# Batched matmul on one core: groups of four matrices, one DMA queue for loads and stores, transposes of 32-bit pairs

## The chip, the cores and the metric

The kernel runs on one core of a Trainium2 chip. A core has a matrix engine (TensorE, "PE" in the profile), a vector engine (VectorE, "DVE"), a scalar engine (ScalarE, "ACT"), GpSimd ("POOL") and a sync engine (SyncE, "SP"), and 16 DMA engines that move data between HBM and the on-chip memory SBUF. Matmul results appear in PSUM, from where DVE or ACT copies them to SBUF. The metric is the device time of one execution in microseconds; the median of nine executions is given for the kernel before.

## What is computed

For each of 8 x 16 = 128 pairs of matrices the kernel forms one product of a 256 x 512 matrix with a 512 x 384 matrix, all in float32 in HBM:

```python
b1, b2, m, k, n = 8, 16, 256, 512, 384
x:      (b1, b2, m, k) float32
weight: (b1, b2, k, n) float32
return np.matmul(x, weight).astype(np.float32)
```

That is 67.1 MB of `x`, 100.7 MB of `weight` and 50.3 MB of output, 218.1 MB in all.

## The kernel before

The 128 products are worked off in groups: 63 groups of two matrices and, at the end, two groups of one. `GX` is 2, so one load of `x` always covers two matrices: `load_x` (line 58) brings 512 rows of `x` as 128 partitions with `R` = 4 consecutive rows each, which is one contiguous run of 8 KB per partition. `load_w` (line 65) brings one weight matrix as 128 partitions with four consecutive rows each, a run of 6 KB per partition. Because partition `p` of the weight tile holds rows 4p to 4p+3, the contraction is split by residue: step `ko` of the matmul takes the rows `ko`, `ko+4`, and so on. `x` is sliced in the same way (`ko::KO` on line 83).

TensorE needs `x` with the contraction on the partitions, so `transpose_x` (line 70) does three things per load: VectorE casts the float32 tile to bf16 (`x_bf`, line 77), TensorE transposes 128 x 128 blocks of it into PSUM (`pt`, line 82), and VectorE copies those to SBUF (`x_t`, line 86). The weights are cast to bf16 by VectorE (`w_bf`, line 110). In the main loop the two matrices of a group share the columns of the matrix engine: each matmul (line 124) has 64 columns of `x_t` as its stationary operand, matrix 0 writes partitions 0 to 63 of `po` and matrix 1 partitions 64 to 127. ScalarE copies `po` to `out_sb` (line 131), where each partition now holds `RG` = 4 consecutive output rows, a run of 6 KB.

The order of the work is set by the queues. All loads are issued from SP in program order. Stores are issued from ACT (`store`, line 95), and a list `waiting` holds each store back until `LAG` = 3 more groups have been computed. The framework gives DMAs eight completion semaphores in turn, so each DMA on SP also waits for the one that used the same semaphore before it: eight DMAs are under way at most, six loads and two stores in the steady state. Buffers are pools: three for the `x` tile, six for the weight tile, six for the output, two PSUM tiles for transposes and three for results. Each engine works off its own instructions in order; the framework has interleaved the instructions of neighbouring groups on VectorE and TensorE.

Of the kernel before, what the change touches and what calls it, by code (L numbers as in the profile page):

```python
# [1 line left out]

# [5 lines left out]


@with_exitstack
def kernel(
    ctx: ExitStack,
    tc: tile.TileContext,
    x: bass.AP,
    weight: bass.AP,
    out: bass.AP,
):
    nc = tc.nc
    P = 128  # L20

    b1, b2, M, K = x.shape
    _, _, _, N = weight.shape
    B = b1 * b2
    KO = K // P

    x_rows = x.rearrange("b1 b2 m k -> (b1 b2 m) k")
    o_rows = out.rearrange("b1 b2 m n -> (b1 b2 m) n")
    w_flat = weight.rearrange("b1 b2 k n -> (b1 b2) k n")

    fp32 = mybir.dt.float32
    bf16 = mybir.dt.bfloat16

    GX = 2
    CX = P // GX
    R = GX * M // P


    groups = [2] * ((B - GX) // 2) + [1] * GX

    LAG = 3

    const = ctx.enter_context(tc.tile_pool(name="const", bufs=1))
    x_pool = ctx.enter_context(tc.tile_pool(name="x_pool", bufs=3))
    xb_pool = ctx.enter_context(tc.tile_pool(name="xb_pool", bufs=2))
    xt_pool = ctx.enter_context(tc.tile_pool(name="xt_pool", bufs=2))
    w_pool = ctx.enter_context(tc.tile_pool(name="w_pool", bufs=6))
    wb_pool = ctx.enter_context(tc.tile_pool(name="wb_pool", bufs=4))  # L50
    out_pool = ctx.enter_context(tc.tile_pool(name="out_pool", bufs=LAG + 3))
    psum_t = ctx.enter_context(tc.tile_pool(name="psum_t", bufs=2, space=bass.MemoryType.PSUM))
    psum_o = ctx.enter_context(tc.tile_pool(name="psum_o", bufs=3, space=bass.MemoryType.PSUM))

    identity = const.tile([P, P], bf16)
    make_identity(nc, identity)

    def load_x(b):
        x_sb = x_pool.tile([P, R, K], fp32, name="x_sb")
        nc.sync.dma_start(  # L60
            x_sb[:], x_rows[b * M : (b + GX) * M].rearrange("(p r) k -> p r k", r=R)
        )
        return x_sb

    def load_w(b):
        w_sb = w_pool.tile([P, KO, N], fp32, name="w_sb")
        nc.sync.dma_start(w_sb[:], w_flat[b].rearrange("(kp ko) n -> kp ko n", ko=KO))  # L67
        return w_sb

    def transpose_x(x_sb, RG):  # L70


        H = R // RG
        x_bf = xb_pool.tile([P, R, K], bf16, name="x_bf")
        x_t = xt_pool.tile([P, RG, KO, P, H], bf16, name="x_t")
        for r0 in range(0, R, 4):
            nc.vector.tensor_copy(out=x_bf[:, r0 : r0 + 4], in_=x_sb[:, r0 : r0 + 4])  # L77
            for r in range(r0, r0 + 4, 2):
                pt = psum_t.tile([P, 2, KO, P], bf16, name="pt")
                for rr in range(2):  # L80
                    for ko in range(KO):
                        nc.tensor.transpose(  # L82
                            pt[:, rr, ko, :], x_bf[:, r + rr, ko::KO], identity
                        )
                j = r % RG
                nc.vector.tensor_copy(  # L86
                    out=x_t[:, j : j + 2, :, :, r // RG], in_=pt[:]
                )
        return x_t

    waiting = []

    def store():
        dram, out_sb = waiting.pop(0)
        nc.scalar.dma_start(out=dram, in_=out_sb)

    b = 0
    for n, G in enumerate(groups):
        last = n == len(groups) - 1
        C = P // G  # L100
        RG = G * M // P
        if b % GX == 0:
            x_sb = load_x(b)
        w_sb = [load_w(b + i) for i in range(G)]
        if b % GX == 0:
            x_t = transpose_x(x_sb, RG)
        w_bf = []
        for i in range(G):
            t = wb_pool.tile([P, KO, N], bf16, name="w_bf")
            nc.vector.tensor_copy(out=t[:], in_=w_sb[i][:])  # L110
            w_bf.append(t)
        if last:
            while waiting:
                store()

        out_full = out_pool.tile([P, 2 * M // P, N], fp32, name="out_sb")
        out_sb = out_full[:, :RG]
        for r in range(0, RG, 2):
            po = psum_o.tile([P, 2, 512], fp32, name="po")
            for rr in range(2):  # L120
                for ko in range(KO):
                    for i in range(G):
                        c0 = (b % GX + i) * CX
                        nc.tensor.matmul(  # L124
                            po[i * C : (i + 1) * C, rr, :N],
                            x_t[:, r + rr, ko, c0 : c0 + CX, :],
                            w_bf[i][:, ko, :],
                            start=(ko == 0),
                            stop=(ko == KO - 1),
                        )  # L130
            nc.scalar.copy(out=out_sb[:, r : r + 2, :], in_=po[:, :, :N])  # L131
        waiting.append(
            (
                o_rows[b * M : (b + G) * M].rearrange("(p r) n -> p r n", r=RG),
                out_sb,
            )
        )
        if len(waiting) > LAG or last:
            store()
        b += G  # L140


# [1 line left out]
_INS = ['x', 'weight']  # L144
_OUTS = [((8, 16, 256, 384), 'float32')]


# [23 lines left out]
```

## Time and profile before

| | |
|---|---|
| median of 9 executions | 531.84 us (530.17 to 534.15) |
| the profiled execution's own time | 530.17 us |
| its span in the profile | 528.0 us |
| PE busy | 346.8 us (66%) |
| DVE busy | 277.7 us (53%) |
| ACT busy | 103.8 us (20%) |
| granted TensorE clock, mean | 0.853 |
| HBM traffic over the span | 413 GB/s (167.77 MB read, 50.33 MB written) |

The span is the part of the execution that the profiler covers, from the first instruction to the last; the execution's own time is 2.17 us longer. Busy times are those of each engine on its own, and they overlap. A line of the profile that begins with a line number, an engine and an operation stands for a group of instructions of that kind: how many, their busy time, the mean of one in nanoseconds, and then how long the engine was idle just before them and what released it.

### The profile page before, as it was taken

What the parts mean: (1) busy time and instruction counts of PE and PEld (TensorE: products, weight loads), DVE (VectorE), ACT (ScalarE), POOL (GpSimd) and SP (SyncE); (2) the same over time, 40 slices, a digit from 0 to 9 for tenths busy, and PEclk for the clock granted to TensorE, in tenths of its full rate; (3) what the DMA queues carried; (4) which work ended last, traced back from release to release, by engine and by line L of the source; (5) the groups of instructions that cost most, each with busy time, mean ns of one, the idle gap of its engine ahead of it and who ended that gap; (6) DMA issues with size and microseconds to landing.
All of it is one profiled execution on the core that took longest, in us unless ns stands there. A gap on an engine that the chain in (4) does not pass through costs nothing.

```text
span 528.0 us, 7363 instructions
## 1 busy us (share of the span) xinstructions
PE 346.8 (66%) x3056; PEld 235.9 (45%) x3056; DVE 277.7 (53%) x320; ACT 103.8 (20%) x129; POOL 0.7 (0%) x6
## 2 busy tenths in 40 slices
PE   4685566675765766657667666576575775766664
PEld 2454344444543544445435444444454443544443
DVE  4545545555465545554654555546555455455464
ACT  0212111221211212212212122122221221112112
POOL 0000000000000000000000000000000000000000
PEclk9969888888788878887888888878888788788789
DMA  8999999999999999999999999999999999999994
GB/s 343 405 424 422 425 421 421 425 421 422 423 421 425 420 420 426 421 422 423 421 424 423 419 424 421 422 425 421 422 422 422 422 422 425 419 426 421 424 411 192
DMA packets 37041, 218.59 MB, mean 414 GB/s; under 512 B 4112, under 2 KB 4112, under 8 KB 28816
## 3 DMA queue, kind: packets, MB, share of 16 engines
q1 hardware_dynamic: 27648, 167.78, 76.4%
q10 hardware_dynamic: 9360, 50.34, 23.0%
q8 instruction: 24, 0.39, 0.3%
q14 instruction: 9, 0.07, 0.0%
HBM read 167.77 MB, written 50.33 MB: 413 GB/s over the span
## 4 chain that ended last, share of the span: by engine, by line
DMA 75%; PE 15%; DVE 8%; issue 1%; ACT 0%; SPq 0%; DVEq 0%
DMA w_sb<-in_weight_dram 75%; PE po L124 13%; DVE w_bf L110 5%; DVE x_t L86 3%; PE pt L82 2%; ACT out_sb L131 0%; SPq L60 0%; DVEq L110 0%; SPq L67 0%
## 5 line engine op out<-in xcount | busy, mean ns | idle before, releaser
L124 PE MATMUL po<-w_bf,x_t 128*64 128x384 bf16 (+1 forms) x2032 | 279.5, 411 | 164.1 <-DVE w_bf L110 163.3
L124 PEld LDWEIGHTS <-x_t 128*64 128x64 bf16 (+1 forms) x2032 | 175.6, 136 | 252.2 <-DVE w_bf L110 127.4
L131 ACT COPY out_sb<-po 128x768 f32<-128x768 f32 x128 | 102.5, 801 | 420.2 <-PE po L124 420.2
L77 DVE CAST x_bf<-x_sb 128x2048 bf16<-128x2048 f32 x64 | 78.5, 1227 | 136.4 <-DMA x_sb<-in_x_dram 136.4
L110 DVE CAST w_bf<-w_sb 128x1536 bf16<-128x1536 f32 x128 | 119.6, 954 | 26.8 <-DMA w_sb<-in_weight_dram 26.0
L86 DVE COPY x_t<-pt 128x1024 bf16<-128x1024 bf16 x128 | 83.6, 695 | 81.3 <-PE pt L82 81.3
L82 PE MATMUL pt<-identity,x_bf 128*128 128x128 bf16 x1024 | 70.3, 222 | 13.0 <-DVE x_bf L77 12.9
L82 PEld LDWEIGHTS <-x_bf 128*128 128x128 bf16 x1024 | 60.2, 115 | 35.4 <-DVE x_bf L77 27.0
L131 ACT ACT_TABLE_LOAD x1 | 1.3, 1283 | 0.7 <-PEq L155 0.7
masks.py:199 POOL TENSOR_SCALAR_AFFINE_SELECT identity<-identity 128x128 bf16<-128x128 bf16 x1 | 0.3, 292 | 0.1
masks.py:197 POOL MEMSET identity<- 128x128 bf16 x1 | 0.2, 204 | 0.3 <-POOLq L155 0.3
L155 POOL MEMSET const-bfloat16-1.0<- 128x1 bf16 x1 | 0.1, 101 | 0.0
L155 POOL MEMSET const-uint8-127<- 128x1 uint8 x1 | 0.1, 101 | 0.0
L155 POOL MEMSET const-float32-0.0<- 128x1 f32 x1 | 0.1, 98 | 0.2 <-issue 0.2
L155 POOL MEMSET const-float32-1.0<- 128x1 f32 x1 | 0.1, 98 | 0.0
## 6 DMA issues: line engine op xcount, KB each, us to landing
w_sb<-in_weight_dram SPq DMA_DIRECT2D x128, 768.0 KB, 16.2
x_sb<-in_x_dram SPq DMA_DIRECT2D x64, 1024.0 KB, 16.1
out_dram<-out_sb ACTq DMA_DIRECT2D x63, 768.0 KB, 8.3
out_dram<-out_sb ACTq DMA_DIRECT2D x2, 384.0 KB, 2.3
```

The costliest lines, as they stand in the source:

```text
L77: nc.vector.tensor_copy(out=x_bf[:, r0 : r0 + 4], in_=x_sb[:, r0 : r0 + 4])
L82: nc.tensor.transpose(pt[:, rr, ko, :], x_bf[:, r + rr, ko::KO], identity)
L86: nc.vector.tensor_copy(out=x_t[:, j : j + 2, :, :, r // RG], in_=pt[:])
L110: nc.vector.tensor_copy(out=t[:], in_=w_sb[i][:])
L124: nc.tensor.matmul(po[i * C : (i + 1) * C, rr, :N], x_t[:, r + rr, ko, c0 : c0 + CX, :], w_bf[i][:, ko, :], start=(ko == 0), stop=(ko == K ...
L131: nc.scalar.copy(out=out_sb[:, r : r + 2, :], in_=po[:, :, :N])
L155: nc = _bacc.Bacc("TRN2", target_bir_lowering=False, num_devices=1)
```

## The change

Groups become four matrices, 32 groups in all. One load of `x` covers four matrices: 128 partitions with `R` = 8 rows each, a run of 16 KB. A partition of a group's output also holds 8 consecutive rows of one matrix, a run of 12 KB, so a matrix occupies a quadrant of 32 partitions of `x_sb` and of `out_sb`. Stores are issued from SP instead of ACT, each behind the loads of a group that lies two groups (of four) later. The weight pool has eight buffers, the `x` pool two, the output pool four. In the last group the two waiting stores are issued right behind the loads, and each matrix gets a store of its own.

The transposes take pairs of bf16 values as one 32-bit word: the bf16 tile is viewed as float32, and one 128 x 128 transpose of words moves 256 values per row; half as many transposes are needed. The copy from PSUM (line 85 of the new kernel) reads the words as bf16 again and writes `x_t` in runs of 64 values, and the matmul picks one of the two values of a pair with a step of two. The stationary operand is now 128 columns of one matrix (line 117), so each result tile `po` has the 256 output rows of one matrix, spread over the partitions such that quadrant `g` holds rows of residue class `g`. Four copies per matrix, each from one quadrant of `po` to the quadrant of `out_sb` that belongs to the matrix, put them in place (line 127): three by ScalarE, one by VectorE.

```diff
-    GX = 2
-    CX = P // GX
-    R = GX * M // P
+    G = 4
+    C = P // G
+    R = G * M // P
+    J = R // G
-    groups = [2] * ((B - GX) // 2) + [1] * GX
-    LAG = 3
+    LAG = 2
-    x_pool = ctx.enter_context(tc.tile_pool(name="x_pool", bufs=3))
+    x_pool = ctx.enter_context(tc.tile_pool(name="x_pool", bufs=2))
-    w_pool = ctx.enter_context(tc.tile_pool(name="w_pool", bufs=6))
+    w_pool = ctx.enter_context(tc.tile_pool(name="w_pool", bufs=8))
-    out_pool = ctx.enter_context(tc.tile_pool(name="out_pool", bufs=LAG + 3))
+    out_pool = ctx.enter_context(tc.tile_pool(name="out_pool", bufs=4))
-    identity = const.tile([P, P], bf16)
+    identity = const.tile([P, P], fp32)
...
-    def transpose_x(x_sb, RG):
+    def transpose_x(x_sb):
-        H = R // RG
         x_bf = xb_pool.tile([P, R, K], bf16, name="x_bf")
-        x_t = xt_pool.tile([P, RG, KO, P, H], bf16, name="x_t")
+        x_t = xt_pool.tile([P, J, KO // 2, G, G, C, 2], bf16, name="x_t")
+        words = x_bf[:].bitcast(fp32)
         for r0 in range(0, R, 4):
             nc.vector.tensor_copy(out=x_bf[:, r0 : r0 + 4], in_=x_sb[:, r0 : r0 + 4])
             for r in range(r0, r0 + 4, 2):
-                pt = psum_t.tile([P, 2, KO, P], bf16, name="pt")
+                pt = psum_t.tile([P, 2, KO // 2, P], fp32, name="pt")
                 for rr in range(2):
-                    for ko in range(KO):
+                    for h in range(KO // 2):
                         nc.tensor.transpose(
-                            pt[:, rr, ko, :], x_bf[:, r + rr, ko::KO], identity
+                            pt[:, rr, h, :], words[:, r + rr, h :: KO // 2], identity
                         )
-                j = r % RG
+                j, g = divmod(r, G)
                 nc.vector.tensor_copy(
-                    out=x_t[:, j : j + 2, :, :, r // RG], in_=pt[:]
+                    out=x_t[:, j, :, :, g : g + 2].rearrange(
+                        "k h i g c e -> k g (h i) (c e)"
+                    ),
+                    in_=pt[:].bitcast(bf16).rearrange(
+                        "k g h (i ce) -> k g (h i) ce", i=G
+                    ),
                 )
...
-        nc.scalar.dma_start(out=dram, in_=out_sb)
+        nc.sync.dma_start(out=dram, in_=out_sb)
...
+    for b in range(0, B, G):
+        last = b == B - G
+        x_sb = load_x(b)
         w_sb = [load_w(b + i) for i in range(G)]
         if last:
             while waiting:
                 store()
+        x_t = transpose_x(x_sb)
+        out_sb = out_pool.tile([P, R, N], fp32, name="out_sb")
+        for i in range(G):
+            w_bf = wb_pool.tile([P, KO, N], bf16, name="w_bf")
+            nc.vector.tensor_copy(out=w_bf[:], in_=w_sb[i][:])
+            po = psum_o.tile([P, J, 512], fp32, name="po")
+            for j in range(J):
                 for ko in range(KO):
+                    nc.tensor.matmul(
+                        po[:, j, :N],
+                        x_t[:, j, ko // 2, i, :, :, ko % 2].rearrange("k g c -> k (g c)"),
+                        w_bf[:, ko, :],
+                        start=(ko == 0),
+                        stop=(ko == KO - 1),
+                    )
+            mine = slice(i * C, (i + 1) * C)
+            for g in range(G):
+                copy = nc.vector.tensor_copy if g == i else nc.scalar.copy
+                copy(out=out_sb[mine, g::G, :], in_=po[g * C : (g + 1) * C, :, :N])
+            if last:
+                waiting.append((o_rows[(b + i) * M : (b + i + 1) * M].rearrange(
+                    "(p r) n -> p r n", r=R), out_sb[mine]))
+                store()
+        if not last:
+            waiting.append(
+                (o_rows[b * M : (b + G) * M].rearrange("(p r) n -> p r n", r=R), out_sb[:])
+            )
+            if len(waiting) > LAG:
+                store()
```

The removed main loop is the one shown with the kernel before. As built, VectorE's order per group of the new kernel is: two `x` casts, weight cast 0, two copies of transposes, weight cast 1, two copies of transposes, weight cast 2, output copies 0 and 1, weight cast 3, output copies 2 and 3. TensorE's is the 16 transposes, then the 32 matmuls. SP's is one `x` load, four weight loads and one store.

More of the change, by code (lines that the diff above doesn't have):

```diff
@@ L60, in load_x @@
         nc.sync.dma_start(
-            x_sb[:], x_rows[b * M : (b + GX) * M].rearrange("(p r) k -> p r k", r=R)
+            x_sb[:], x_rows[b * M : (b + G) * M].rearrange("(p r) k -> p r k", r=R)
         )
@@ L94, in store @@
         dram, out_sb = waiting.pop(0)
[L95 to L103, printed above, removed]
-        w_sb = [load_w(b + i) for i in range(G)]
[L105 to L111, printed above, removed]
+        nc.sync.dma_start(out=dram, in_=out_sb)
+    for b in range(0, B, G):
+        last = b == B - G
+        x_sb = load_x(b)
+        w_sb = [load_w(b + i) for i in range(G)]
         if last:
@@ L114 @@
                 store()
[L116 to L120, printed above, removed]
-                for ko in range(KO):
[L122 to L135, printed above, removed]
-            )
[L137 to L140, printed above, removed]
+        x_t = transpose_x(x_sb)
[5 more added lines that the diff above has]
+            for j in range(J):
+                for ko in range(KO):
+                    nc.tensor.matmul(
[13 more added lines that the diff above has]
+                store()
```

## The prediction

> **What bounds the kernel now.** First the page's totals, slices and queues:
>
> ```profile
> span 528.0 us, 7363 instructions
> ...
> PE 346.8 (66%) x3056; PEld 235.9 (45%) x3056; DVE 277.7 (53%) x320; ACT 103.8 (20%) x129; POOL 0.7 (0%) x6
> ...
> DMA  8999999999999999999999999999999999999994
> GB/s 343 405 424 422 425 421 421 425 421 422 423 421 425 420 420 426 421 422 423 421 424 423 419 424 421 422 425 421 422 422 422 422 422 425 419 426 421 424 411 192
> ...
> q1 hardware_dynamic: 27648, 167.78, 76.4%
> q10 hardware_dynamic: 9360, 50.34, 23.0%
> ```
>
> No compute engine is busy above 66%; the DMA engines are busy in every slice, at 422 GB/s, and the shares of loads (q1) and stores (q10) add to 99%. The chain of waits agrees:
>
> ```profile
> DMA 75%; PE 15%; DVE 8%; issue 1%; ACT 0%; SPq 0%; DVEq 0%
> ```
>
> SP waits almost only for DMAs, not for buffers that computing frees:
>
> ```profile
> SPq L67 <- DMA w_sb<-in_weight_dram: 254.9, 123, 4.1
> SPq L60 <- DMA x_sb<-in_x_dram: 172.4, 61, 4.0
> ...
> SPq L67 <- DVE w_bf L110: 3.3, 16, 0.2
> ```
>
> The busy times by stretch give steady state and edges (length; PE, PEld, DVE, ACT, POOL; clock, DMA share, GB/s):
>
> ```profile
> 13.20:26.40 13.20, 8.45 (x86) 5.78 (x84) 7.27 (x9) 3.20 (x4) 0.00 (x0) 0.93 1.02 405
> 26.40:500.00 473.60, 315.93 (x2798) 215.16 (x2796) 251.00 (x290) 92.90 (x116) 0.00 (x0) 0.85 1.02 422
> 500.00:514.80 14.80, 10.73 (x92) 7.06 (x90) 8.50 (x10) 3.21 (x4) 0.00 (x0) 0.80 0.99 412
> ```
>
> All 218.59 MB at 422.3 GB/s would take 517.6 us. The shortfall of the first two slices (79 and 17 GB/s for 13.2 us) is 3.0 us, that of the end (10 GB/s for 14.8 us, 229 for 13.2) 7.5 us: 528.1, the span. So the bound is the rate of the DMA engines plus two edges.
>
> The rate comes from single packets. In the trace's DMA records (medians) a 6144-byte packet takes 234 ns, an 8192-byte one 309, a 3072-byte one 122 and the 4-byte packet that ends a DMA 9. The line through them is 9 ns per packet plus 36.6 ps per byte.
>
> Last, the groups that the change touches (mean ns of one after the busy time):
>
> ```profile
> L124 PE MATMUL po<-w_bf,x_t 128*64 128x384 bf16 (+1 forms) x2032 | 279.5, 411 | 164.1 <-DVE w_bf L110 163.3
> L131 ACT COPY out_sb<-po 128x768 f32<-128x768 f32 x128 | 102.5, 801 | 420.2 <-PE po L124 420.2
> L77 DVE CAST x_bf<-x_sb 128x2048 bf16<-128x2048 f32 x64 | 78.5, 1227 | 136.4 <-DMA x_sb<-in_x_dram 136.4
> L110 DVE CAST w_bf<-w_sb 128x1536 bf16<-128x1536 f32 x128 | 119.6, 954 | 26.8 <-DMA w_sb<-in_weight_dram 26.0
> L86 DVE COPY x_t<-pt 128x1024 bf16<-128x1024 bf16 x128 | 83.6, 695 | 81.3 <-PE pt L82 81.3
> L82 PE MATMUL pt<-identity,x_bf 128*128 128x128 bf16 x1024 | 70.3, 222 | 13.0 <-DVE x_bf L77 12.9
> ```
>
> **What the Trainium skill says.** "DMA: Bandwidth & Descriptors", "Why small descriptors are slow", gives each packet a fixed cost of about 3 cycles on an internal bus; the line above shows 9 ns per packet, so the direction agrees. The same page, "Issuing engines are not separate DMA queues", says that moving an issue between engines saves only sequencer time; in the packet records, stretches with loads alone ran at 421 GB/s and those with half stores at 423 to 424, which agrees within 0.6%. "TensorE: Matmul & The Clock Gate", "Terms", says that a transpose mode makes float32 transposes 4 times faster; no float32 transpose is in the trace before. "VectorE: DVE Perf Modes", "The perf-mode tier table", lets a copy from PSUM run two elements per cycle for bf16 and one for float32: line 86 agrees (1024 in 695 ns), a float32 copy from PSUM on VectorE is not shown.
>
> **The change, part by part.** The unit is four matrices (6.82 MB; 32 such). Its time today is 6.82 MB / 422.3 GB/s = 16.14 us.
>
> *Longer runs and fewer DMAs.* Each of 16 DMA engines has, before, 16 x packets of 309 ns, 32 w of 234, 16 out of 234 and 8 closing ones of 9: 16.25 us. After: 8 x of 16 KB (estimate from the line: 609 ns), the same w, 8 out of 12 KB (459), 6 closing: 16.09 us. That is 1.0% less. On 517.6 us: -5.2 us, and a unit then takes 15.98 us. If the fixed part weren't per packet the gain would be 0; it cannot exceed this by much.
>
> *Stores on SP.* A store is one issue of 0.34 us on ACT in the timeline (last of the lines below), a load 0.33 on SP; six issues per 16 us are 2 us of SP. New is the wait: on SP, store n-2 stands behind the loads of group n and ahead of those of n+1, so a late store would hold loads back. By the eight semaphores it goes out when w2 of group n-1 has landed, 26.6 us after group n-2's x load began to move (16.0 for a unit, 4.9 for x, three w of 1.9). By the loop below its output copies end about 21 us after that start (4.9 for x, 6.9 of VectorE work, 7.1 of matmuls, 2.4 for ScalarE's last three copies). Cover: 5 us, and behind it seven DMAs are in flight, about 18 us of traffic. Cost 0; buffers likewise, since x and w of n-2 are cast one unit before their slots are wanted.
>
> *VectorE.* Casts stay. The 128 copies of transposes stay at 695 ns if bf16 pairs still move two per cycle (runs of 64; unit step). One output copy per matrix is added: 768 float32 from PSUM. From lines 77 and 110, 0.533 ns per element at two per cycle; at one, 768 x 1.067 + 0.14 = 0.96 us. Per unit 2 x 1.23 + 4 x 0.95 + 4 x 0.70 + 4 x 0.96 = 12.9 us of 16.
>
> *ScalarE.* From 4 copies per unit to 12 of 0.80 us (a copy's time goes by elements per partition, still 768): 9.6 us of 16, hidden.
>
> *TensorE.* The timeline has the bursts (start, length, engine, operation, count):
>
> ```profile
> 509.40 0.80 ACT L131 COPY out_sb<-po 128x768 f32<-128x768 f32 x1 [5.60 <-PE po L124]
> 510.64 1.08 PE L82 MATMUL pt<-identity,x_bf 128*128 128x128 bf16 x16
> 521.12 2.77 PE L124 MATMUL po<-w_bf,x_t 128*128 128x384 bf16 x16 [2.95 <-DVE w_bf L110]
> 524.76 0.34 ACTq L95 DMA_DIRECT2D out_dram<-out_sb  x1
> ...
> 212.24 4.93 PE L124 MATMUL po<-w_bf,x_t 128*64 128x384 bf16 x32 [1.80 <-DVE w_bf L110]
> ```
>
> 32 transposes become 16 of float32. 16 bf16 ones take 1.08 us here, 0.07 each; bounds 0.07 and 4 x 0.12 = 0.5 us, taken 0.15. The matmuls are 32 instead of 64; the last group before already ran 128 columns, 16 in 2.77 us, 0.173 each, as much as a pair of 64-column ones. At the half clock the burst of 32 narrow ones took 4.93 us, 0.31 per pair.
>
> *Does computing keep pace?* The queue orders make a loop: after the last matmul of a group, output copy 3 (0.96), two x casts (2.46), w cast (0.95), two transpose copies (1.29 as a pair), w cast (0.95), two copies (1.29), hand-overs 0.3, then 28 of the matmuls: 8.2 us + 28 m. At full clock 13.0 us, at half clock 16.9. The trace's clock record switches in stretches of 3.41 us and left the half clock only after a stretch of back-to-back matmuls. With 8 quiet us per group I expect about 16 matmuls at half clock and 12 at full: 5.0 + 2.1, loop 15.3 us. That is 0.7 us under 15.98: DMA stays the bound, narrowly. Cost 0.
>
> *Edges.* Start: x and w reach 8 DMAs at once; part of the 0.5 us lost in the second slice goes, -0.3. End: after the last weights land, two held stores (7.4 us) still move while ScalarE empties its last copies, about 11 us after that landing, then a quarter store of about 2.3 us (as its 384 KB counterpart before): some 14 us in which 11 us worth of data moves, and closing time; 6.5 us lost against 7.5: -1.0.
>
> Sum: 528.0 - 5.2 - 0.3 - 1.0 = 521.5 span, + 2.17 = 523.7 for such an execution, 1.2% under its 530.17. The median stood 1.67 us above that execution: 525.3.
>
> **Rivals.** *A, slower: VectorE and TensorE's loop becomes the bound*, from 16.0 us per group on. For it: only 0.7 us of cover, and unknown transposes and layouts. If line 85's copies fall to one element per cycle (+0.5 us each, four in the loop), 17.4; float32 transposes of 0.5 us expose about 2.5 us, 17.8. Each us above 16.0 costs 32 us: 17.1 on average, about 560; range 535 to 600. Against it: bf16 with unit step, and work may lag two groups. *B: the packet gain is absent*, the limit being elsewhere: only the edges remain, 530.5. Against it: 122, 234 and 309 ns lie on one line. *C: one ring is worse*, 64 changes between loads and stores at 0.3 us each: 545. Against it: loads alone already ran one ring at 421.
>
> **How the numbers follow.** Forecast 0.60 (its own range 519 to 530), A 0.25, B 0.10, C 0.05. A difference under 0.2% can't be told from none. Faster: 0.60 + 0.06 of B; same: 0.04 of B; slower: A + C = 0.30. The range 519 to 556 holds the forecast, B, C and the lower part of A (0.10), some 0.8.
>
> **What would show it.** Right: 425 to 428 GB/s in the middle slices, packets near 609 and 459 ns, SP waiting for DMAs, VectorE about 78% busy and waiting for x. Wrong: DMA slices below 9, SP waiting for VectorE, line 85 well over 0.7 us, the transposes over 0.3 us, or w packets above 236 ns.

## The result, and the profile after

The changed kernel takes 663.7 us in the median of 10 runs (662.03 to 664.89), against 531.82 for the kernel before (32 runs on the same chips). The ratio is 1.2471 [1.2452, 1.2489]. The forecast was 525.3 and the range ended at 556.

The page of the kernel after: totals, then the slices.

```profile
span 661.6 us, 4583 instructions
...
PE 333.5 (50%) x1536; PEld 215.0 (33%) x1536; DVE 393.7 (60%) x448; ACT 304.4 (46%) x385; POOL 0.7 (0%) x6
...
DMA  9999999778978879778797877987879878789324
GB/s 361 418 423 423 424 421 388 314 326 342 374 312 319 328 317 396 312 316 323 317 400 314 319 316 324 376 336 310 324 317 365 356 311 315 327 342 372 135 96 95
```

No compute engine is busy for more than 60% of the span, and the DMA engines are no longer full either: after six slices (about 100 us) their rate falls from 420 to between 310 and 400 GB/s. Stretches show the same (start and end, length, busy time of PE, PEld, DVE, ACT and POOL, clock, DMA share, GB/s):

```profile
26.00:76.00 50.00, 29.56 (x136) 19.21 (x136) 35.48 (x41) 23.72 (x31) 0.00 (x0) 0.76 1.02 425
120.00:600.00 480.00, 241.94 (x1113) 156.43 (x1114) 289.29 (x329) 221.57 (x281) 0.00 (x0) 0.75 0.83 332
```

At first the kernel moves 425 GB/s, what the prediction hoped for, and from 120 us on 332, with the DMA engines 83% busy. Loads run ahead into free buffers at the start; how far these carry the higher rate isn't shown here.

SP's waits say who holds the transfers back (line of the waiting instruction, what it waited for, us in total, times, longest):

```profile
SPq L99 <- DVE out_sb L127: 253.0, 33, 20.1
SPq L66 <- DVE w_bf L113: 212.7, 87, 4.5
...
SPq L66 <- DMA w_sb<-in_weight_dram: 11.5, 8, 1.5
```

Before, SP waited for DMAs (254.9 and 172.4 us). Now it waits for VectorE: for its output copies and for its casts, which free the input buffers. So computing sets the pace. The costliest groups (busy time, mean ns of one, then the idle time before them and what ended most of it):

```profile
L127 DVE COPY out_sb<-po 32x768 f32<-32x768 f32 x128 | 122.1, 954 | 251.8 <-ACT out_sb L127 206.8
L81 PE MATMUL pt<-identity,x_bf 128*128 128x128 f32 x512 | 126.8, 427 | 252.6 <-DVE x_bf L76 228.6
...
L85 DVE COPY x_t<-pt 128x1024 bf16<-128x1024 bf16 x128 | 85.2, 686 | 1.4
```

VectorE's own work has the size that was predicted (copies of transposes 686 ns, output copies 954). What wasn't predicted is the end of the first line: VectorE stands idle for 206.8 us in front of its output copies until *ScalarE* has finished output copies. Since no data passes from one output copy to another, this is a wait that the change itself does not name. One group in the timeline (start, length, engine, line, operation, count, idle time before it and its releaser):

```profile
308.16 0.96 DVE L127 COPY out_sb<-po 32x768 f32<-32x768 f32 x1 [2.28 <-ACT out_sb L127]
...
309.15 2.36 DVE L76 CAST x_bf<-x_sb 128x2048 bf16<-128x2048 f32 x2
...
310.44 1.98 PE L81 MATMUL pt<-identity,x_bf 128*128 128x128 f32 x8 [7.27 <-DVE x_bf L76]
...
314.94 5.21 PE L117 MATMUL po<-w_bf,x_t 128*128 128x384 bf16 x24
...
318.23 0.95 DVE L127 COPY out_sb<-po 32x768 f32<-32x768 f32 x1 [1.49 <-PE po L117]
318.93 9.68 ACT L127 COPY out_sb<-po 32x768 f32<-32x768 f32 x12 [10.80 <-issue]
319.75 0.95 DVE L127 COPY out_sb<-po 32x768 f32<-32x768 f32 x1 [0.57 <-ACT out_sb L127]
...
325.40 0.95 DVE L127 COPY out_sb<-po 32x768 f32<-32x768 f32 x1 [3.71 <-ACT out_sb L127]
328.64 0.96 DVE L127 COPY out_sb<-po 32x768 f32<-32x768 f32 x1 [2.28 <-ACT out_sb L127]
...
329.63 2.36 DVE L76 CAST x_bf<-x_sb 128x2048 bf16<-128x2048 f32 x2
```

Read it from the top. Output copy 3 of the group before ends at 309.12, and only then do the `x` casts start: they stand behind it in VectorE's queue. Transposes and matmuls follow, and copy 0 starts 9.08 us after the start of the casts. ScalarE starts 0.70 later, on twelve copies without a gap (9.68 us). VectorE's copy 2 starts at 325.40, when ScalarE's eighth has ended (318.93 + 8 x 0.807 = 325.39), and copy 3 at 328.64, when the twelfth has (328.61). Then the next `x` casts. The loop has 0.98 + 9.08 + 0.70 + 9.68 and hand-overs: 20.48 us, of which a unit's DMA traffic needs 16.

The program says which copy waits, once one knows that the copies of one matrix wait for each other. The ScalarE copies of matrix *i* with `g` below *i*, of which there are *i*, stand ahead of VectorE's copy in the program, and VectorE's waits for them. For copy 2 they are copies 7 and 8 of ScalarE's twelve; for copy 3 they are copies 9, 10 and 12, the copies of the last two matrices being interleaved there.

The whole time follows from that loop. The first `x` cast starts at 8.5 us and those of the last group at 636.8: 31 loops of 20.27 us in the mean. After those the kernel needs 24.8 us more: 8.5 + 628.3 + 24.8 = 661.6, the span.

The first two of these loops are shorter, 17.3 us, and they show what the place of copy 3 is worth. The `x` casts stand ahead of it there; from the third group on the order is the other one, and every later loop takes 20.4 to 20.5 us:

```profile
42.11 0.95 DVE L127 COPY out_sb<-po 32x768 f32<-32x768 f32 x1 [4.70 <-ACT out_sb L127]
43.09 2.36 DVE L76 CAST x_bf<-x_sb 128x2048 bf16<-128x2048 f32 x2
45.49 0.96 DVE L127 COPY out_sb<-po 32x768 f32<-32x768 f32 x1
...
59.27 0.95 DVE L127 COPY out_sb<-po 32x768 f32<-32x768 f32 x1 [4.70 <-ACT out_sb L127]
62.51 0.96 DVE L127 COPY out_sb<-po 32x768 f32<-32x768 f32 x1 [2.28 <-ACT out_sb L127]
63.50 2.36 DVE L76 CAST x_bf<-x_sb 128x2048 bf16<-128x2048 f32 x2
```

At 43.09 the casts follow copy 2; at 63.50 they follow copy 3, which has waited for four more of ScalarE's copies.

### The profile page after: what moved, and what is told of

Same layout as the page of the kernel before. It is cut to its first block, busy times and chain, and to the rows that moved or that the text cites. A ratio compares the mean times of both kernels' runs of the same rounds, so it can differ in the third digit from the quotient of the medians.

```text
span 661.6 us, 4583 instructions
## 1 busy us (share of the span) xinstructions
PE 333.5 (50%) x1536; PEld 215.0 (33%) x1536; DVE 393.7 (60%) x448; ACT 304.4 (46%) x385; POOL 0.7 (0%) x6
## 2 busy tenths in 40 slices
DMA packets 27719, 218.40 MB, mean 330 GB/s; under 512 B 3120, under 2 KB 3120, under 8 KB 19504
## 5 line engine op out<-in xcount | busy, mean ns | idle before, releaser
L127 ACT COPY out_sb<-po 32x768 f32<-32x768 f32 x384 | 303.1, 789 | 351.2 <-issue 302.5
L127 DVE COPY out_sb<-po 32x768 f32<-32x768 f32 x128 | 122.1, 954 | 251.8 <-ACT out_sb L127 206.8
L81 PE MATMUL pt<-identity,x_bf 128*128 128x128 f32 x512 | 126.8, 427 | 252.6 <-DVE x_bf L76 228.6
L117 PE MATMUL po<-w_bf,x_t 128*128 128x384 bf16 x1024 | 213.3, 370 | 65.2 <-ACT out_sb L127 65.2
L81 PEld LDWEIGHTS pt<-identity,x_bf 128*128 128x128 f32 x512 | 101.2, 222 | 277.4 <-DVE x_bf L76 230.7
L117 PEld LDWEIGHTS <-x_t 128*128 128x128 bf16 x1024 | 114.3, 112 | 158.5 <-issue 107.1
L113 DVE CAST w_bf<-w_sb 128x1536 bf16<-128x1536 f32 x128 | 121.7, 952 | 0.9
L85 DVE COPY x_t<-pt 128x1024 bf16<-128x1024 bf16 x128 | 85.2, 686 | 1.4
L76 DVE CAST x_bf<-x_sb 128x2048 bf16<-128x2048 f32 x64 | 75.6, 1222 | 9.5 <-DMA x_sb<-in_x_dram 8.5
```

The costliest lines, as they stand in the source:

```text
L81: nc.tensor.transpose(pt[:, rr, h, :], words[:, r + rr, h :: KO // 2], identity)
L85: nc.vector.tensor_copy(out=x_t[:, j, :, :, g : g + 2].rearrange("k h i g c e -> k g (h i) (c e)"), in_=pt[:].bitcast(bf16).rearrange("k g ...
L113: nc.vector.tensor_copy(out=w_bf[:], in_=w_sb[i][:])
L117: nc.tensor.matmul(po[:, j, :N], x_t[:, j, ko // 2, i, :, :, ko % 2].rearrange("k g c -> k (g c)"), w_bf[:, ko, :], start=(ko == 0), stop= ...
L127: copy(out=out_sb[mine, g::G, :], in_=po[g * C : (g + 1) * C, :, :N])
```

## The experiments

Three theories on the 132 us. **W**: VectorE's output copies wait for ScalarE's copies of the same matrix, and what stands behind them in VectorE's queue is late. **S**: the stores, waiting on SP for output copies, hold the loads back. **T**: the 32-bit transposes, with their layouts and the half clock, make the loop long. Ratios are to the kernel before on the same chip; a time without one is a single run.

**VectorE's copy first.** One line of the changed kernel: of each matrix's four output copies, VectorE's comes first in the program. The work is the same.

```diff
-            for g in range(G):
+            for g in [i] + [g for g in range(G) if g != i]:
```

> Of the four output copies of a matrix VectorE's is put first in the program, ScalarE's three after it; nothing else changes. Theory W (the copies of a matrix wait for each other in program order, since they write interleaved rows of the same partitions, so that VectorE's copies 2 and 3 end behind ScalarE's twelve): VectorE then waits for TensorE alone, a group's loop falls from 20.5 us to the 15 to 16 us of VectorE and TensorE, the DMA engines are the bound again and the time is 518 to 532 us. Rival T (the float32 transposes, 0.25 us apart, and the half clock make the loop long): the transposes are untouched, so at least 640 us. Rival S (stores on SP hold the loads behind them back): the stores stay on SP, so at least 640 us.

Measured: 528.61 us, ratio 0.9942 [0.9922, 0.9962]. The whole loss is gone. Two waits and the middle stretch of this run:

```profile
ACT out_sb L127 <- DVE out_sb L127: 212.1, 32, 16.9
...
DVE out_sb L127 <- PE po L117: 85.2, 64, 2.4
```

```profile
26.00:500.00 474.00, 299.61 (x1433) 189.38 (x1432) 366.37 (x418) 280.69 (x356) 0.00 (x0) 0.81 1.01 424
```

The wait has turned round: ScalarE, which has 40% of its time to spare, waits for VectorE, and VectorE's output copies wait only for products (its `x` casts wait for loads, 34.4 us in all). DMA is the bound again. From the first `x` cast (8.5) to those of the last group (502.37) a loop takes 15.93 us, and 24.8 us follow them, the same as in the changed kernel: 31 x (20.27 - 15.93) = 134.5 us, all of the difference between the two spans (134.4).

**All output copies on ScalarE.** This takes VectorE, the second reader of the result tile, away altogether, and with it 3.8 us of VectorE's work per loop.

```diff
-                copy = nc.vector.tensor_copy if g == i else nc.scalar.copy
+                copy = nc.scalar.copy
```

> All four output copies of a matrix are ScalarE's, 16 per group; VectorE has none. Theory W: no wait between the two engines is left on the output tile, ScalarE is busy 16 x 0.79 = 12.6 us per group, VectorE 9 us, both under the 16.0 us of the DMA engines: 518 to 535 us. A variant of it, ScalarE's work in line with the rest of the loop (ScalarE's last copy frees the result tiles that the next group's matmuls need), would leave 550 to 640 us. Rival T: unchanged, at least 640 us. Rival S: at least 640 us.

Measured: 530.70 us, ratio 0.9984 [0.9967, 1.0001]. ScalarE is now busy for 406.0 us of 528.9, more than any engine in the changed kernel, and still the loss is gone. So ScalarE's work was not the cost. Since VectorE's work changed too, it is the first experiment, with the work kept, that shows the wait between the two engines to be the cost.

**Stores from ScalarE's queue.** The part of the change that S blames is undone alone.

```diff
-        nc.sync.dma_start(out=dram, in_=out_sb)
+        nc.scalar.dma_start(out=dram, in_=out_sb)
```

> The changed kernel with its stores issued from ScalarE's queue instead of SP, nothing else. Rival S: SP is free to run ahead with loads, so the time falls to 520 to 580 us. Theory W: computing sets the pace whoever issues the stores; 655 to 680 us, the upper end because 0.34 us per store is added to ScalarE, which stands in the loop.

Measured: 565.81 us. W missed, and the number lies where S expected it. The timeline shows why it is no evidence for S (VectorE, one group):

```profile
316.58 0.95 DVE L127 COPY out_sb<-po 32x768 f32<-32x768 f32 x1 [4.71 <-ACT out_sb L127]
317.57 2.36 DVE L76 CAST x_bf<-x_sb 128x2048 bf16<-128x2048 f32 x2
319.96 0.96 DVE L127 COPY out_sb<-po 32x768 f32<-32x768 f32 x1
```

Copy 2 still waits 4.71 us for ScalarE. But the next group's `x` casts now stand *ahead* of copy 3: the framework, which decides the order of independent instructions, places them differently once the stores sit in another queue. So copy 3's wait is off the loop, which takes 17.12 us in the mean. The casts then stand as in the first two loops of the changed kernel, and the length is nearly theirs. It still holds a wait of the kind that W names, since it runs through ScalarE's first eight copies and then copy 2: 0.99 us from copy 2 to the casts, 9.61 from there to ScalarE's first copy (300.50 to 310.11) and 6.47 for eight copies are 17.07 us. This experiment changed two things, and one of them was not in its diff.

**Stores longer held.** S tested with the order kept in the steady loop: stores one group later, one more output buffer.

```diff
-    LAG = 2
+    LAG = 3
...
-    out_pool = ctx.enter_context(tc.tile_pool(name="out_pool", bufs=4))
+    out_pool = ctx.enter_context(tc.tile_pool(name="out_pool", bufs=5))
```

> The changed kernel with each store held one group longer (LAG 3) and five output buffers, so that a store's copies are long done when SP reaches it. Rival S (stores waiting on SP hold the loads back and that sets the pace): SP no longer waits for output copies and the time falls to 540 to 600 us. Theory W (the loop of VectorE and ScalarE sets the pace, SP's wait only shows it): SP waits elsewhere, for casts, and the time stays at 650 to 668 us.

Measured: 660.18 us. SP's waits:

```profile
SPq L59 <- DVE x_bf L76: 266.0, 29, 11.6
...
SPq L99 <- DVE out_sb L127: 38.2, 4, 20.1
```

The wait in front of the stores fell from 253.0 to 38.2 us, and came back as a wait of the `x` loads for casts. SP is not the cause; it only shows that VectorE is late. The short loops at the start are three here instead of two.

**Stores from ScalarE's queue, `x` casts forced behind copy 3.** The other half: the queue as in the third experiment, and the `x` casts behind copy 3 as in the changed kernel. Two small copies make the casts depend on the last output copy; the casts then overwrite what they wrote.

```diff
-        nc.sync.dma_start(out=dram, in_=out_sb)
+        nc.scalar.dma_start(out=dram, in_=out_sb)
...
+        if before is not None:
+            for r0 in range(0, R, 4):
+                nc.vector.tensor_copy(out=x_bf[P - C :, r0, :2], in_=before[P - C :, G - 1, :2])
```

> The kernel with stores from ScalarE's queue (565.8 us) plus two tiny VectorE copies per group (32 x 2 values, from the last output rows of the group before into the x tile, overwritten by the cast), which force the x casts behind output copy 3 of the group before, as the changed kernel has them; in the 565.8 us kernel they stand ahead of it. Theory W with order (what the stores on SP changed is the place of the x casts, and behind copy 3 they lie behind ScalarE's twelve copies): 640 to 690 us. Rival S: SP is as free as at 565.8 us, so 560 to 585 us.

Measured: 641.51 us. VectorE:

```profile
323.39 0.96 DVE L131 COPY out_sb<-po 32x768 f32<-32x768 f32 x1 [3.54 <-ACT out_sb L131]
...
324.66 2.36 DVE L79 CAST x_bf<-x_sb 128x2048 bf16<-128x2048 f32 x2
```

With the casts behind copy 3 the loop is 19.55 us in the mean and most of the loss is back, with no store on SP at all. The small copies cost 0.24 us of each loop. The rest of VectorE's order is not that of the changed kernel, and it varies from group to group: in the loop that ends with these lines, the four copies of transposes follow the casts directly, and three weight casts stand behind copy 0. That shortened the path: copy 0 starts 7.52 us after the casts (305.17 to 312.69) instead of 9.08, and then ScalarE's twelve copies (9.69 us) and copy 3 follow as before. S is refuted. The place of the `x` casts against copy 3 accounts for the third experiment, as the first loops of the changed kernel show without any edit.

**bf16 transposes.** The transposes' layout goes back to single bf16 elements (32 per group instead of 16), the rest stays.

```diff
-    identity = const.tile([P, P], fp32)
+    identity = const.tile([P, P], bf16)
...
-                pt = psum_t.tile([P, 2, KO // 2, P], fp32, name="pt")
+                pt = psum_t.tile([P, 2, KO, P], bf16, name="pt")
```

> The changed kernel with bf16 transposes, 32 per group instead of 16 float32 ones, and contiguous columns for the matmuls; groups, copies and queues as in the change. Rival T: transposes at 0.07 us take 1.9 us less per group and the matmuls start sooner, 600 us or less. Theory W: the transposes lie under VectorE's casts except for the first four, so 645 to 668 us.

Measured: 629.13 us, between the two expectations. The loop is 19.19 us instead of 20.27 (1.08 x 31 = 33 us of the 34). VectorE's wait for ScalarE is unchanged, at 207.8 us. Here too the order moved: the four copies of transposes stand differently among the weight casts, so how much of the 1.08 us is due to shorter transposes isn't settled. T holds a part of the loop's length; it isn't the cause that makes it the bound.

**The output tile in four planes.** Why does one copy wait for the other? First guess: they write interleaved rows (`g::G`) of one tile, which are not told apart. Here each `g` writes a plane of its own, and four stores with runs of 1.5 KB put the rows together.

```diff
-        out_sb = out_pool.tile([P, R, N], fp32, name="out_sb")
+        out_sb = out_pool.tile([P, G, J, N], fp32, name="out_sb")
...
-                copy(out=out_sb[mine, g::G, :], in_=po[g * C : (g + 1) * C, :, :N])
+                copy(out=out_sb[mine, g], in_=po[g * C : (g + 1) * C, :, :N])
```

> The changed kernel with the output tile laid out in four planes, one per residue class, so that the four copies of a matrix write rows that do not interleave; each group's store becomes four stores of 1.5 KB runs, which by the packet line cost 0.5 us per group more. If the copies wait for each other because of the rows they write, VectorE's waits for ScalarE vanish and the time is 535 to 570 us. If they wait because they read the same result tile, the waits stay (some 200 us on VectorE) and so does the time, 655 to 690 us.

Measured: 665.66 us, and the wait stays (the list of waits of this run):

```profile
DVE out_sb L128 <- ACT out_sb L128: 207.6, 93, 4.7
```

The guess fell. Sharing the output tile as a whole isn't it either. In the timeline of the changed kernel, VectorE's copy 1 starts when ScalarE's first copy ends (318.93 + 0.807 = 319.74), so that one belongs to matrix 1; it had run beside VectorE's copy 0 (318.23 to 319.18), which writes the same tile. What the copies of one matrix alone share is their source, the result tile `po` in PSUM, and the 32 partitions of the output tile. The source is the likelier; the runs don't separate the two.

**The kernel before with its stores on SP.** The other direction: that part of the change alone.

```diff
-        nc.scalar.dma_start(out=dram, in_=out_sb)
+        nc.sync.dma_start(out=dram, in_=out_sb)
```

> The kernel before with its stores issued from SP, nothing else; VectorE's and TensorE's orders are the same as before. If one ring for loads and stores is worse by itself (the prediction's rival C), slower by 5 us or more; if it is not, within 0.5% of before: 529 to 534 us.

Measured: 528.81 us, ratio 0.9942 [0.9929, 0.9955]. Rival C (one ring, that is, one engine's DMA queue for loads and stores, is worse) is refuted; one ring gains 0.6%.

**VectorE's copy first, stores from ScalarE's queue.** The same question where the runs are long: the first and the third edit together.

> The kernel with VectorE's copy first (528.6 us), with its stores from ScalarE's queue again. If the single ring is what gained 0.5% in the kernel before, this loses it: 530 to 534 us. If it doesn't matter with long runs, 527 to 530 us.

Measured: 532.19 us, ratio 1.0013 [1.0000, 1.0027]; without the second edit it was 528.61, so one ring is worth 0.7% here.

**The kernel before with 16 KB runs of x.** The packet term alone, with stores in either queue.

```diff
-    GX = 2
+    GX = 4
```

> The kernel before with one x load per four matrices (GX = 4: 16 KB runs, 32 x loads instead of 64; the last four matrices are groups of one), all else as before, stores on ACT. Packet line of the prediction: x costs each DMA engine 8 x 609 instead of 16 x 309 ns per four matrices, and one closing packet less per pair, 0.08 us, 32 times 2.6 us: 527.5 to 530.5 us, if the two single groups more at the end cost under 1 us. Packet gain absent: 531 to 533 us.

> Both: GX = 4 and the stores on SP, in the kernel before. The two gains are in different places (packets; start and order of the DMAs), so they add: 525 to 528 us. If they are one and the same slack, 528 to 529.5 us.

Measured: 533.05 us with stores from ScalarE's queue (1.0017 [1.0001, 1.0034]) and 530.50 from SP (0.9965 [0.9950, 0.9980]). Both missed, being slower than their counterparts with 8 KB runs (531.82 and 528.81). With one ring the rate did rise, from 423.1 to 424.4 GB/s between 60 and 480 us in the trace's DMA records; with two it stayed (422.3 and 422.2). What was gained is lost at the end: with four matrices cast at once the last `x` casts start 23.7 us before the end of the span, with two 15.8 (one ring both times). The one ring itself gains again, 2.55 us.

Where does it gain? Three pairs differ in this alone, and in each the last `x` cast starts earlier with one ring: 511.6 against 515.6 us (kernel before), 503.5 against 507.1 (VectorE first), 505.2 against 508.8 (16 KB runs). The spans differ by 0.6, 3.0 and 3.1 us. (The 0.6 is small because the one profiled execution, 530.17 us, is the fastest of its series and the other, 529.53, lies above its median; the medians of that pair lie 2.8 apart.) A part can come from the order of the same bytes: with one ring the held stores stand behind the last loads, with two they share the engines with them. In the second pair that would have to be nearly all, since the rates between 60 and 480 us are 424.1 and 423.9 GB/s. In the others the rate is higher too with one ring (423.1 against 422.3, 424.4 against 422.2). The runs don't divide the gain further.

**Two attempts at a faster version.** First the end: with VectorE's copy first, VectorE takes a second copy of each matrix in the last group.

```diff
-            for g in range(G):
-                copy = nc.vector.tensor_copy if g == i else nc.scalar.copy
+            for g in [(i + d) % G for d in range(G)]:
+                mate = last and g == (i + 1) % G
+                copy = nc.vector.tensor_copy if g == i or mate else nc.scalar.copy
```

> The kernel with VectorE's copy first (528.6 us), and in the last group two of four copies per matrix on VectorE instead of one, so that ScalarE's run of copies after the last weights falls from 12 to 8. If ScalarE's last twelve copies stand ahead of the last stores, the end gets 3 us shorter: 524 to 527.5 us. If the held stores fill that time, no change: 528 to 529 us.

Measured: 531.45 us, ratio 0.9993 [0.9981, 1.0004]. Missed: six copies came to stand in a row ahead of the last weight cast, which started at 516.56 instead of 514.26 us. The load was evened on the two engines, and the queue was made worse.

Second, VectorE's copy first together with bf16 transposes (the edits of the first experiment and of the bf16 one).

> The kernel with VectorE's copy first (528.6 us), with bf16 transposes. There the DMA engines set the pace at 424 GB/s; a loop shorter by about 1 us per group has nothing to win: 526.5 to 530 us. If the float32 transposes still hold its loads up at times, below 526 us.

Measured: 526.89 us, ratio 0.9912 [0.9875, 0.9950]: the fastest version here, under both kernels. The DMA engines run at 424 GB/s in the steady stretch and at 420 in the last slice but one (402 with VectorE's copy first alone). The last group's `x` casts start at 502.45 us, no earlier than there (502.37); the spans differ by 2.2 us, and all of that lies behind those casts, 22.6 us against 24.8. VectorE's order moved here as well, so that the shorter transposes alone did this isn't shown.

## Why the prediction was wrong

**The step that failed** is "Does computing keep pace?", with the clause on *ScalarE*: "9.6 us of 16, hidden". The loop was added up along VectorE and TensorE as 15.3 us. ScalarE's share was taken as hidden since it is only 9.6 us of busy time in 16. But VectorE's copies 2 and 3 wait for ScalarE's copies, and the next `x` casts stand behind copy 3, so ScalarE's whole row is *in* the loop: 20.48 us measured. The durations that the step used held (casts 1.22 and 0.95 us, copies of transposes 0.69, output copies 0.95). So did its sum for a loop without that wait: with VectorE's copy first, while the loads were still ahead, one loop in the steady order took 14.45 us (casts at 37.71 and 52.16). What was missing is a wait between two engines. Why the framework makes the copies wait stays open, as the planes show. Two of the signs of being wrong that were named came: DMA slices below 9, and SP waiting for VectorE.

**Rival A** named the right place and side, with the threshold (16.0 us per group) right. Its price was wrong. It counted slower copies on line 85 (measured 686 ns, no slower than before) and transposes of 0.5 us (measured 8 in 1.98 us at half clock, 0.247 each). The first didn't come, and the second at about half its size: the run with bf16 transposes gained 1.08 us per loop, part of it perhaps by its order. The wait came instead, and the time was 100 us past A's 560.

**Packets.** Right one by one: in the trace's DMA records a 16 KB packet takes 611 ns in the median (609 forecast), 12 KB 460 with VectorE's copy first (459). Wrong in the sum: with VectorE's copy first, 424.1 GB/s (60 to 480 us, DMA records) against 422.3 before is 0.4%, not 1.0%. Two terms that were held fixed moved. The weights' packets, 46% of the bytes, took 236 ns instead of 234, which is 0.4% of the total; and packets overlapped less, their time being 1.012 of the engines' time instead of 1.015, which is 0.3%. Why they did so is open.

**Stores on SP** at cost 0: right for the transfers, and even 0.6% pessimistic. Wrong in that the queue also moved VectorE's order: in the third experiment the `x` casts stood ahead of copy 3 and the span was 564.0 us, with the casts forced behind it 639.7, the stores being on ScalarE's queue in both.

**VectorE's new copy.** Right: 0.954 us (0.96 forecast). The Trainium skill, "VectorE: DVE Perf Modes", "The perf-mode tier table" (its part "Why PSUM operands drop a tier"), on which that rested, agrees with this trace for both kinds: float32 from PSUM at one element per cycle, bf16 at two (1024 in 686 ns).

**TensorE.** 0.15 us per float32 transpose was taken; at full clock 8 take 1.23 us with VectorE's copy first, 0.154 each. At half clock 8 take 1.98, 0.247 each, which was not priced. Both figures share out the end of the last one; from start to start it is 0.120 and 0.213. Matmuls: 8 in 1.46 us, 0.18 each, forecast 0.173.

**Edges.** A gain of 1.3 us was forecast. With VectorE's copy first, where they can be seen, the span of 527.2 less 218.40 MB at 424.1 GB/s (515.0) leaves 12.2; before, by the same sum, 528.0 - 517.6 = 10.4. The edges got 1.8 us longer. In the forecast's own sum for the end, 14 us less 11 us of data leave 3 us; the closing time that makes it 6.5 was not worked out.

**The odds.** What the forecast priced, and what it called the likeliest, is what the kernel does with one line in another order: 528.61, still 3.3 us above it. Even there it is in part luck: of its terms the longer runs were to bring 5.2 us and the single ring nothing, but with the stores back in ScalarE's queue the same kernel takes 532.19 (1.0013), no less than before, and the ring makes the difference.

## What to carry to other kernels

When two engines empty one result tile, look for waits between them, in the program's order and in the trace, before adding up busy times: an engine that is 46% busy can sit on the critical loop, as ScalarE did here. Put first, in the program, the copy of the engine that the loop runs through, so that the other one waits. And after any edit of a queue compare the order of instructions on every engine: the edit that is in the diff may not be the one that moved the time.

## What was not expected of the hardware

- One DMA ring for loads and stores was faster than two by 0.5 to 0.7% in three pairs. The last `x` cast started 3.6 to 4.0 us earlier in each, and the rate rose by 0.2 to 0.5% in two of them; how the gain divides is open.
- Longer runs pay little. 16 KB and 12 KB runs raised the steady rate by 0.4% where the single packets (611 ns for 16 KB against twice 309 for 8 KB, 460 for 12 KB against twice 234) promised 1.0%; 16 KB runs of `x` alone left it unchanged with two rings.
- A float32 transpose of 128x128 takes 0.154 us at full clock and 0.247 at half (bursts of eight), against 0.07 for a bf16 one in the kernel before (a burst of sixteen): per element of bf16 about the same at full clock. From start to start it is 0.120 and 0.213, against 0.056.
